# Early transposed tiles of a hybrid decoder layer: Newton steps on GpSimd, smaller pieces, and the next load behind the transposes

## The chip, the core and the metric

The kernel runs on one core of a Trainium2 chip. The core has five engines with queues of their own: TensorE (PE, matrix products; PEld is its weight load), VectorE (DVE), ScalarE (ACT), GpSimd (POOL) and SyncE (SP, which here only starts DMA transfers; ACT and POOL start some too). The metric is the device time of one execution in microseconds, lower is better. "Profile" is one execution recorded by the hardware profiler.

## The reference

One layer of a decoder with 2048 prompt rows and 8 sample rows of width 1024. A row is normalized by the root of its mean square, multiplied by a gain and shifted by a modulation worked out from a condition vector; then one input projection, a gated linear recurrence (LRU) group beside a gated linear attention (GLA) group of four heads, an output projection, a gate, the residual and a last normalization:

```
ada = jax.nn.silu(c) @ w_ada + b_ada
shift, scale, gate = jnp.split(ada, 3, axis=-1)
hn = _rmsnorm(x, g_norm) * (1.0 + scale[:, None]) + shift[:, None]
z = hn @ w_in
xa, za, q, k, v, glr, zg = jnp.split(z, SPLITS, axis=-1)
...
mix = jnp.concatenate([y_lru, y_gla], axis=-1) @ w_out
x = x + gate[:, None] * mix
```

What matters here is `hn`, and in it only the rows 1024 to 2047.

## The kernel before

The prompt is worked in two halves of 1024 rows. The first half's normalized rows lie on chip as a high and a low part (`hh`, `hl`), transposed, so that products can be made in three matmuls (L388 to L390 for the values of a head, L703 to L705 for all other projections, in `project`). A head of GLA makes the values of eight row tiles (`values`; ACT copies the high part out of the accumulator at L999, DVE subtracts for the low part at L1000, after which the accumulator is free; there are four accumulators), then keys and queries in two segments, with the decay (L1015 to L1054) between, the products of keys and queries (L1084 reads what DVE multiplies at L1069), and two segments of gates. An LRU tile makes two projections in segments (`xa_unit`, `za_unit`), with a convolution (L1321), a SiLU (L1172 on ACT, L1173 on DVE) and a scan (L1366 to L1377) at its end. The order in the first half is: head 3; LRU tile 0; head 0; LRU tiles 1, 2; head 1; LRU tiles 3, 4; head 2; LRU tiles 5, 6, 7.

**The early tiles.** While the first half is projected, the eight row tiles of the second half are made ready by `turn_ahead` (L263). It takes one tile of 128 rows at a time: load from memory (L266), sum of squares on ACT (L167), inverse root (`scales`, which calls `rsqrt`, L149 to L155: three preparing steps and three Newton rounds of three steps each, on one column), scaling of the rows (`times`, L183), transposes of 32 by 32 blocks into a second buffer (L277), a multiplication and an addition with the modulation (L284), and four stores to memory (L289). Both buffers come from a pool of two (`xt`). When the second half begins, `hn_load` (L296) reads all tiles back and `modulate` (L197, with L208 on POOL and L209 on DVE) splits them into high and low parts.

**What sets their order.** `after(units, f)` puts `f` on a list that is due so many units later; `tick` moves the clock, by 1 after a projection of a segment and by 0.5 after a row tile's values, and calls all that is due, in order of due time. A step that comes due between two ticks waits for the next. The tile steps are chained so: squaring 3 units after the load, scaling with transposes 0.5 later, both modulations 0.5 later, stores 0.5 later, and then the next tile's load. `behind(V)` (L723) keeps an instruction behind the last one traced on DVE so far. Beyond that, a scheduler at build time draws up each engine's queue: what is traced earlier goes first, but an instruction whose inputs are ready may pass earlier ones that are not.

In the same stretch of time other work hangs on the same clock: `pair_weights` (differences of weight blocks on DVE at L819 and L825, copies on ACT at L824, stores and loads by POOL at L827 and L815), then `out_weights` (L858, L893, loads and stores by POOL at L872 and L907), and the splitting of projection weights (L346 on ACT, L347 on DVE, stored by SP at L364). `apply` (L219), which works on the first rows, runs its copy on POOL (L229) and its subtraction on DVE (L232).

Of the kernel before, what the change touches and what calls it, by code (L numbers as in the profile page):

```python
# [8 lines left out]
F32 = mybir.dt.float32  # L9
# [3 lines left out]
OP = mybir.AluOpType  # L13

P = 128
D = 1024
KT = D // P
T = 2048
TH = T // 2
NS = 8  # L20
# [34 lines left out]
def hybrid_kernel(ctx, tc, i, o):  # L55
    nc = tc.nc
    V, S, G, PE, SP = nc.vector, nc.scalar, nc.gpsimd, nc.tensor, nc.sync
# [30 lines left out]
    xp = p1.enter_context(tc.tile_pool(name="xp", bufs=2))  # L88
# [52 lines left out]
                    mybir.DependencyClass.NoSync, mybir.DependencyReason.DATA), reason="in_order")  # L141
            last[x.engine] = x

    def rsqrt(pool, out, ss, n, rows, scale):

        y = pool.tile([P, 16], F32, tag="rs_y", name="rs_y", bufs=1)[:rows, :n]
        t = pool.tile([P, 16], F32, tag="rs_t", name="rs_t", bufs=1)[:rows, :n]
        x = pool.tile([P, 16], F32, tag="rs_x", name="rs_x", bufs=1)[:rows, :n]
        V.tensor_scalar(x, ss, scale, EPS, op0=OP.mult, op1=OP.add)  # L149
        V.tensor_scalar(t.bitcast(I32), x.bitcast(I32), 1, None, op0=OP.logical_shift_right)  # L150
        V.tensor_scalar(y.bitcast(I32), t.bitcast(I32), -1, 0x5F3759DF, op0=OP.mult, op1=OP.add)
        for it in range(3):
            V.tensor_tensor(t, y, y, op=OP.mult)
            V.scalar_tensor_tensor(t, t, -0.5, x, op0=OP.mult, op1=OP.mult)
            V.scalar_tensor_tensor(out if it == 2 else y, t, 1.5, y, op0=OP.add, op1=OP.mult)  # L155
# [9 lines left out]
    def square_sum(pool, out, x, m, n, tag="f512"):  # L165
        junk = pool.tile([P, 1024], mybir.dt.bfloat16, tag=tag, name="junk", bufs=2)
        S.activation(junk[:m, :n], x, AF.Square, accum_out=out)  # L167

    def squares(pool, xt, m=P, tag="f512", ss=None, j0=0):
        if ss is None:  # L170
            ss = pool.tile([P, 4], F32, tag="ss", name="ss", bufs=2)
        for j, x in enumerate(xt, j0):
            square_sum(pool, ss[:m, j:j + 1], x[:m], m, D, tag)
        return ss

    def scales(pool, ss, n, m=P):
        rs = pool.tile([P, 4], F32, tag="rs", name="rs", bufs=2)
        rsqrt(pool, rs[:m, :n], ss[:m, :n], n, m, 1.0 / D)
        return rs

    def times(xt, rs, m=P, j0=0):
        for j, x in enumerate(xt, j0):
            V.tensor_scalar(x[:m], x[:m], rs[:m, j:j + 1], None, op0=OP.mult)  # L183

    def normalize(pool, xt, m=P, tag="f512"):

        times(xt, scales(pool, squares(pool, xt, m, tag), len(xt), m), m)
# [74 lines left out]

    def turn_ahead(q, gm):  # L263

        x, w = [xp.tile([P, TH + NS], F32, tag="xt", name="xt")[:, :D] for _ in range(2)]
        SP.dma_start(x, i["x_prompt"][0, TH + q * P:TH + (q + 1) * P])  # L266

        def squared():
            ss = squares(xp, [x])
            after(0.5, lambda: scaled(ss))  # L270

        def scaled(ss):
            with behind(V):
                times([x], scales(xp, ss, 1))
                for h in range(2):
                    y, z = [v[:, 512 * h:512 * h + 512] for v in (w, x)]
                    V.transpose(y.rearrange("p (c k j) -> p c k j", c=4, k=4), z.rearrange("p (k c j) -> p c k j", c=4, k=4))  # L277
            after(0.5, modulated)

        def modulated():  # L280
            w3 = w.rearrange("p (b j) -> p b j", j=32)
            with behind(V):
                for n, op in enumerate((OP.mult, OP.add)):
                    V.tensor_tensor(w3, w3, gm[:, n, :, None].to_broadcast([P, 32, 32]), op=op)  # L284
            after(0.5, stored)

        def stored():
            for a in range(4):
                SP.dma_start(fd[q // 4, :, :, 4 * (q % 4) + a].rearrange("h (c r) f -> r (h c) f", c=4),  # L289
                             w[32 * a:32 * a + 32].rearrange("r (b f) -> r b f", b=8))  # L290
            if q < 7:
                turn_ahead(q + 1, gm)

        after(3, squared)

    def hn_load():  # L296

# [138 lines left out]
    rows = st.tile([NROW, D], F32, tag="rows", name="rows")  # L436
# [167 lines left out]
    def first_head():  # L604
# [29 lines left out]
        with in_order():  # L634
            ranks = []
            ss = squares(st, xt0[4:6], P, "junk")
            split_parts(1)
            rs = scales(st, ss, 2)
            split_parts(1)
            times(xt0[4:6], rs)  # L640
# [82 lines left out]
    def behind(q):  # L723

        return tc.issue_after(next(x for x in reversed(list(nc.cur_bb.bb.instructions)) if x.engine == q.engine))
# [17 lines left out]
    def after(units, fn, gla=False, val=False):  # L743
        clock[1] += 1
        heapq.heappush(pend, (clock[0] + units, clock[1], fn, gla, val))
# [17 lines left out]
    def ada_gate():  # L763

        pg = acc()

        def step(kt):
            ws = [xp.tile([P, TH + NS], F32, tag="xt", name="xt")[:, :D] for _ in range(2)]
            for n, w in enumerate(ws):
                SP.dma_start(w, i["w_ada"][0, (kt + n) * P:(kt + n + 1) * P, 2 * D:])  # L770

            def mm():
                for n in (1, 0):
                    for g in range(4):
                        PE.matmul(pg[32 * g:32 * g + 32, :256], sc[:, kt + n], ws[n][:, g * 256:(g + 1) * 256],
                                  start=kt == 0 and n == 1, stop=kt == KT - 2 and n == 0)
                if kt + 2 < KT:
                    step(kt + 2)
                else:
                    gr = xp.tile([P, 512], F32, tag="f512", name="gr")[:, :256]  # L780
                    S.copy(gr, pg[:, :256])
                    SP.dma_start(gated, gr)
                    after(4, lambda: ready("gate"))
                    turn_ahead(0, spread_modulation())
            after(3, mm)

        step(0)
# [339 lines left out]
    def gla_norm(nch, run):  # L1127
        _, on, ss = run
        rs = gp.tile([P, 4], F32, tag="ors", name="ors")
        rsqrt(gp, rs[:, :nch], ss[:, :nch], nch, P, 1.0 / DV)  # L1130
        for c in range(nch):
            V.tensor_scalar(on[:, c], on[:, c], rs[:, c:c + 1], None, op0=OP.mult)
# [21 lines left out]
    def sample_out(h, qm, s0, done):  # L1154

        os_ = gp.tile([P, DV], F32, tag="os", name="os")
        po = psum.tile([P, 512], F32, tag="o", name="po", bufs=1)[:, :DV]
        for m in range(2):
            for n in (3, 0, 1, 2):
                PE.matmul(po[32 * n:32 * n + 32], qm[:, 4 * m + n], s0[m][:, n], start=m == 0, stop=m == 1)  # L1160
        for m in range(2):
            G.dma_start(o[7][0, 4 * m:4 * m + 4, h].rearrange("b k v -> k b v"), s0[m])
        V.tensor_copy(os_, po)
        ss = gp.tile([P, 4], F32, tag="oss2", name="oss2")
        rs = gp.tile([P, 4], F32, tag="ors2", name="ors2")
        square_sum(xp, ss[:, :1], os_, P, DV)
        rsqrt(gp, rs[:, :1], ss[:, :1], 1, P, 1.0 / DV)
        V.tensor_scalar(os_, os_, rs[:, :1], None, op0=OP.mult)
        done(os_)
# [1047 lines left out]
    for n in range(2, 16):  # L2217
        g = n - 1
        x, prev = pairs[n], pairs[n - 1]
# [81 lines left out]
```

## Time and profile before

| | |
|---|---|
| median of 3 runs | 1453.01 us (1451.71 to 1453.09) |
| the profiled execution | 1452.74 us |
| its span, from the first to the last instruction | 1450.5 us |
| granted clock of TensorE, mean | 0.995 |
| instructions | 23542 |

A page of the profile gives busy times by engine and the costliest groups of instructions by line. Other views of the same trace give the waits of an engine (whom it waited for, total us, times, longest us) and the timeline: start in us from the span's start, duration in us, engine, line, operation, written and read tiles, shape, count, and in brackets the idle time of the engine just before, with what ended it. Times of the text are from the span's start.

### The profile page before, as it was taken

Reading aid. Unit: us, or ns where it says so; the run is one execution under the profiler, and the core shown is the slowest. Engines: PE = TensorE matmul, PEld = TensorE weight load, DVE = VectorE, ACT = ScalarE, POOL = GpSimd, SP = SyncE. Lnnn points to the kernel's source line nnn. Section 1 sums busy time; section 2 is a strip of 40 time slices with the busy share of each in tenths; the row PEclk is TensorE's granted clock in tenths of the full one; section 3 lists DMA queues with packets and bytes.
Section 4 is the critical chain, followed back from the end, with each engine's and each line's share of the span. In section 5 each row is a group of like instructions: output and inputs, shape, how many; then the busy total and the mean of one; then the engine's idle time right before and its main releaser. Section 6 shows DMA issues by size and latency. Waiting matters only on the chain.

```text
span 1450.5 us, 23542 instructions
## 1 busy us (share of the span) xinstructions
PE 1418.1 (98%) x8677; PEld 1246.9 (86%) x8677; DVE 1079.9 (74%) x2551; ACT 679.9 (47%) x1227; POOL 220.0 (15%) x362
## 2 busy tenths in 40 slices
PE   8999999989999999999999999999999999999998
PEld 6889989878888988888899999999998887778886
DVE  5757659877888768945458688596888986688886
ACT  4644544654366345524354454635567522144342
POOL 1200111121111114000110422333210000000000
PEclk9999999999999999999999999999999999999999
DMA  9755776885667667567744675665671767694453
GB/s 327 270 185 175 262 248 214 264 270 185 215 199 222 208 200 256 184 241 235 287 149 153 200 247 165 236 196 181 235 250 71 280 225 277 225 359 136 139 168 116
DMA packets 176840, 313.75 MB, mean 216 GB/s; under 512 B 20370, under 2 KB 106034, under 8 KB 173901
## 3 DMA queue, kind: packets, MB, share of 16 engines
q1 hardware_dynamic: 122821, 225.82, 46.0%
q0 software_dynamic: 22912, 70.96, 14.5%
q10 hardware_dynamic: 30992, 15.47, 3.6%
q8 instruction: 68, 1.11, 0.3%
q14 instruction: 47, 0.39, 0.1%
HBM read 192.74 MB, written 119.53 MB: 215 GB/s over the span
## 4 chain that ended last, share of the span: by engine, by line
PE 82%; DVE 9%; ACT 3%; DMA 3%; issue 2%; POOL 0%; DVEq 0%; SPq 0%; ACTq 0%
PE acc L1887 12%; PE acc L703 11%; PE acc L705 11%; PE acc L704 11%; PE tp L1887 9%; PE acc L1601 6%; PE acc L388 4%; PE acc L389 3%; PE acc L390 3%; PE po L1115 2%; DMA w<-parts 1%; DMA wada<-in_w_ada_dram 1%; PE acc L1358 1%; PE tp L1084 1%; PE tp L1206 1%
## 5 line engine op out<-in xcount | busy, mean ns | idle before, releaser
L703 PE MATMUL acc<-hh,w 128*128 128x512 f32 (+3 forms) x1112 | 378.0, 340 | 3.5 <-DVE zs L1173 1.9
L705 PE MATMUL acc<-hh,w 128*128 128x512 f32 (+3 forms) x1112 | 376.5, 339 | 0.0
L704 PE MATMUL acc<-hl,w 128*128 128x512 f32 (+3 forms) x1112 | 375.9, 338 | 0.0
L703 PEld LDWEIGHTS acc<-hh,w 128*128 128x128 f32 x1112 | 210.1, 189 | 21.3 <-issue 3.0
L705 PEld LDWEIGHTS acc<-hh,w 128*128 128x128 f32 x1112 | 210.0, 189 | 16.3
L704 PEld LDWEIGHTS acc<-hl,w 128*128 128x128 f32 x1112 | 210.0, 189 | 15.3
L1887 PE MATMUL acc<-w,a 128*128 128x512 f32 (+1 forms) x792 | 184.8, 387 | 0.0
L1887 PEld LDWEIGHTS acc<-w,a 128*128 128x128 f32 x792 | 146.8, 188 | 33.2 <-issue 3.4
L388 PE MATMUL acc<-w,hh 128*128 128x256 f32 (+1 forms) x508 | 145.0, 286 | 5.6 <-DVE vl L1000 5.4
L390 PE MATMUL acc<-w,hl 128*128 128x256 f32 (+1 forms) x508 | 143.5, 282 | 0.2 <-DVE hl L232 0.2
L389 PE MATMUL acc<-w,hh 128*128 128x256 f32 (+1 forms) x508 | 143.4, 282 | 0.0
L1887 PE MATMUL tp<-w,a 128*128 128x512 f32 x564 | 136.1, 391 | 0.0
L1887 PEld LDWEIGHTS tp<-w,a 128*128 128x128 f32 x564 | 105.2, 188 | 26.9 <-issue 5.2
L388 PEld LDWEIGHTS acc<-w,hh 128*128 128x128 f32 x508 | 96.5, 190 | 7.4 <-DVE vl L1000 6.0
L390 PEld LDWEIGHTS acc<-w,hl 128*128 128x128 f32 x508 | 96.6, 190 | 0.4 <-DVE hl L232 0.4
L389 PEld LDWEIGHTS acc<-w,hh 128*128 128x128 f32 x508 | 96.2, 189 | 0.2
L1172 ACT ACTIVATE zs<-acc 128x512 f32<-128x512 f32 (+3 forms) x70 | 34.3, 490 | 112.6 <-PE acc L705 105.7
L1737 ACT CAST a<-s 128x512 fp32r<-128x512 f32 x61 | 36.5, 620 | 94.7 <-issue 35.2
L1321 DVE SCALAR_TENSOR_TENSOR cv<-xa,vecT,cv 128x512 f32<-128x512 f32 (+2 forms) x120 | 76.2, 639 | 3.5 <-ACT cv L1319 2.9
L1173 DVE SCALAR_TENSOR_TENSOR zs<-zs,acc 128x512 f32<-128x512 f32 (+3 forms) x70 | 38.3, 548 | 35.6 <-ACT zs L1172 35.6
L999 ACT CAST vh<-acc 128x256 fp32r<-128x256 f32 x56 | 20.5, 370 | 87.6 <-PE acc L390 71.9
L1000 DVE TENSOR_TENSOR vl<-acc,vh 128x256 fp32r<-128x256 f32 x56 | 23.2, 418 | 47.0 <-ACT vh L999 46.9
(402 smaller groups left out, 2756.2 us busy)
## 6 DMA issues: line engine op xcount, KB each, us to landing
parts<-w SPq DMA_DIRECT2D x37, 1024.0 KB
w<-parts SPq DMA_DIRECT2D x28, 1024.0 KB
wr<-in_w_in_dram SPq DMA_DIRECT2D x38, 512.0 KB
a<-mixd SPq DMA_DIRECT2D x63, 256.0 KB
w<-wd SPq DMA_DIRECT2D x12, 1024.0 KB
w<-twd SPq DMA_DIRECT2D x20, 512.0 KB
wada<-in_w_ada_dram SPq DMA_DIRECT2D x16, 512.0 KB
mixd<-zs ACTq DMA_DIRECT2D x32, 256.0 KB
```

The source lines that it names most:

```text
L388: PE.matmul(ps, hh[:, kt, c], hi[:, kt % 4], start=kt == 0, stop=False)
L389: PE.matmul(ps, hh[:, kt, c], lo[:, kt % 4], start=False, stop=False)
L390: PE.matmul(ps, hl[:, kt, c], hi[:, kt % 4], start=False, stop=kt == KT - 1)
L703: PE.matmul(ps[:, :n], hi[:, kt], a, start=kt == 0, stop=False)
L704: PE.matmul(ps[:, :n], hi[:, kt], b, start=False, stop=False)
L705: PE.matmul(ps[:, :n], lo[:, kt], a, start=False, stop=kt == KT - 1)
L1172: S.activation(z, ps, AF.Tanh, scale=0.5)
L1173: V.scalar_tensor_tensor(z, z, 1.0, ps, op0=OP.add, op1=OP.mult)
L1321: V.scalar_tensor_tensor(cv[:, cq], xa[:, cq.start + k:cq.stop + k], cw[k], cv[:, cq], op0=OP.mult, op1=OP.add)
L1601: PE.matmul(ps, w[:, u, k], x[v][k], start=start and (k, u, v) == (0, 0, 0), stop=(k, u) == (3, 1), skip_group_check=True)
L1737: S.copy(t[:, 0, k], (low(t) if src is None else src)[:, k])
L1887: PE.matmul(ps, t[:, u, k], w[:, v, k, c], start=(q < 3 or ps is own) and (k, u, v) == (0, 0, 0), stop=(k, u) == (3, 1), skip_group_check= ...
```

## The change

The inverse root gets a parameter for the engine of its Newton rounds; for the early tiles these run on POOL, in four steps a round, where DVE took three. The root is made in the step that squares. The second buffer is taken only when the transposes are due. The step after that scales and transposes, and then starts the next tile (its load). The two modulations become steps of their own, and the stores follow. The distances are 3.5, 0.75, 0.5, 0.5 and 0.5 units.

```
-    def rsqrt(pool, out, ss, n, rows, scale):
+    def rsqrt(pool, out, ss, n, rows, scale, q=V):
...
         for it in range(3):
+            if q is G:
+                G.tensor_tensor(t, y, y, op=OP.mult)
+                G.tensor_tensor(t, t, x, op=OP.mult)
+                G.tensor_scalar(t, t, -0.5, 1.5, op0=OP.mult, op1=OP.add)
+                G.tensor_tensor(out if it == 2 else y, t, y, op=OP.mult)
+                continue
             V.tensor_tensor(t, y, y, op=OP.mult)
             V.scalar_tensor_tensor(t, t, -0.5, x, op0=OP.mult, op1=OP.mult)
             V.scalar_tensor_tensor(out if it == 2 else y, t, 1.5, y, op0=OP.add, op1=OP.mult)
...
     def turn_ahead(q, gm):
-        x, w = [xp.tile([P, TH + NS], F32, tag="xt", name="xt")[:, :D] for _ in range(2)]
+        x = xp.tile([P, TH + NS], F32, tag="xt", name="xt")[:, :D]
         SP.dma_start(x, i["x_prompt"][0, TH + q * P:TH + (q + 1) * P])
 
         def squared():
-            ss = squares(xp, [x])
-            after(0.5, lambda: scaled(ss))
-
-        def scaled(ss):
+            rs = scales(xp, squares(xp, [x]), 1, P, G)
+            after(0.75, lambda: turned(rs))
+
+        def turned(rs):
+            w = xp.tile([P, TH + NS], F32, tag="xt", name="xt")[:, :D]
             with behind(V):
-                times([x], scales(xp, ss, 1))
+                times([x], rs)
                 for h in range(2):
...
-            after(0.5, modulated)
-
-        def modulated():
+            if q < 7:
+                turn_ahead(q + 1, gm)
+            after(0.5, lambda: modulated(w, 0, OP.mult))
+
+        def modulated(w, n, op):
             w3 = w.rearrange("p (b j) -> p b j", j=32)
             with behind(V):
-                for n, op in enumerate((OP.mult, OP.add)):
-                    V.tensor_tensor(w3, w3, gm[:, n, :, None].to_broadcast([P, 32, 32]), op=op)
-            after(0.5, stored)
-
-        def stored():
+                V.tensor_tensor(w3, w3, gm[:, n, :, None].to_broadcast([P, 32, 32]), op=op)
+            after(0.5, (lambda: stored(w)) if n else lambda: modulated(w, 1, OP.add))
+
+        def stored(w):
             for a in range(4):
...
-            if q < 7:
-                turn_ahead(q + 1, gm)
-
-        after(3, squared)
+
+        after(3.5, squared)
```

More of the change, by code (lines that the diff above doesn't have):

```diff
@@ L174, in squares, with scales @@
         return ss
-    def scales(pool, ss, n, m=P):
+    def scales(pool, ss, n, m=P, q=V):
         rs = pool.tile([P, 4], F32, tag="rs", name="rs", bufs=2)
-        rsqrt(pool, rs[:m, :n], ss[:m, :n], n, m, 1.0 / D)
+        rsqrt(pool, rs[:m, :n], ss[:m, :n], n, m, 1.0 / D, q)
         return rs
```

## The prediction

> **What bounds the kernel now.** I read the engines' busy table first, then the waits of TensorE (PE) alone, then the order of time around the two largest of them.
>
> ```profile
> PE 1418.1 (98%) x8677; PEld 1246.9 (86%) x8677; DVE 1079.9 (74%) x2551; ACT 679.9 (47%) x1227; POOL 220.0 (15%) x362
> ```
>
> PE is busy for 98% of a span of 1450.5 us, so about 32 us in all can be gained by anything that leaves the matmuls as they are, and the change leaves them. DVE is at 74%: work taken from it is worth nothing by itself, only where PE stands for it. The early tiles run within 185 to 495 us. PE's waits there:
>
> ```profile
> PE acc L388 <- DVE vl L1000: 5.4, 1, 5.4
> PE tp L1084 <- DVE xb L1069: 3.1, 2, 2.1
> PE acc L1358 <- ACT xh L1345: 0.4, 1, 0.4
> PE acc L1359 <- DVE xl L1346: 0.4, 1, 0.4
> ```
>
> That is 9.3 us. One of the L1084 waits (1.0 us, at 188.73, quoted below with the other) lies ahead of the first tile's work, so 8.3 us is the most that easing the tiles can bring. Two stalls carry it: A, 5.4 us, and B, 2.1 us. Both have an early tile's pieces in front of them. Stall A, on DVE, with the line of ACT and of PE that belong to it:
>
> ```profile
> 286.70 0.69 DVE L1173 SCALAR_TENSOR_TENSOR zs<-zs,acc 128x512 f32<-128x512 f32 x1 [3.33 <-ACT zs L1172]
> 287.31 0.14 DVE L149 TENSOR_SCALAR rs_x<-ss 128x1 f32<-128x1 f32 x1
> ...
> 290.73 0.75 DVE L183 TENSOR_SCALAR xt<-xt,rs 128x1024 f32<-128x1024 f32 x1
> 292.82 1.23 DVE L347 TENSOR_TENSOR w<-wr,w 128x1024 fp32r<-128x1024 f32 x1 [1.34 <-DMA wgr<-in_w_gate_x_dram]
> 293.96 1.30 DVE L277 STREAM_TRANSPOSE xt<-xt 128x512 f32<-128x512 f32 x2
> 295.18 0.65 DVE L819 TENSOR_TENSOR tr<-tr 128x512 f32<-128x512 f32 x1
> ...
> 302.36 1.20 DVE L284 TENSOR_TENSOR xt<-xt,gm 128x1024 f32<-128x1024 f32 x1
> 303.48 0.14 DVE L1380 COPY hc<-tg 128x1 f32<-128x1 f32 x1
> ...
> 304.14 1.21 DVE L284 TENSOR_TENSOR xt<-xt,gm 128x1024 f32<-128x1024 f32 x1
> 305.27 1.28 DVE L825 TENSOR_TENSOR tr<-tr,th 128x512 f32<-128x512 f32 x2
> 306.48 0.41 DVE L1000 TENSOR_TENSOR vl<-acc,vh 128x256 fp32r<-128x256 f32 x1
> ```
>
> ```profile
> 296.47 0.35 ACT L999 CAST vh<-acc 128x256 fp32r<-128x256 f32 x1
> ```
>
> ```profile
> 306.95 0.58 PE L388 MATMUL acc<-w,hh 128*128 128x256 f32 x1 [5.42 <-DVE vl L1000]
> ```
>
> The subtraction that frees the accumulator (306.48) has had its input since 296.8. It is DVE's queue that is late: from 292.82 DVE works without a gap, and in that stretch lie tile 2's transposes and both its modulations. Ahead of it is slack: 3.33 us idle before 286.70 and 1.34 us before 292.82. Stall B:
>
> ```profile
> 327.32 0.14 DVE L149 TENSOR_SCALAR rs_x<-ss 128x1 f32<-128x1 f32 x1
> ...
> 327.88 0.16 DVE L153 TENSOR_TENSOR rs_t<-rs_y 128x1 f32<-128x1 f32 x1
> ...
> 329.62 0.75 DVE L183 TENSOR_SCALAR xt<-xt,rs 128x1024 f32<-128x1024 f32 x1
> 330.41 1.31 DVE L277 STREAM_TRANSPOSE xt<-xt 128x512 f32<-128x512 f32 x2
> 331.64 0.65 DVE L858 TENSOR_TENSOR g<-g,bt 128x512 f32<-128x512 f32 x1
> 332.21 0.68 DVE L1069 SCALAR_TENSOR_TENSOR xb<-acc,xb 128x512 f32<-128x512 f32 x1
> ```
>
> ```profile
> 188.73 1.16 PE L1084 MATMUL tp<-xb,e 128*128 128x128 f32 x8 [0.96 <-DVE xb L1069]
> ...
> 332.94 1.16 PE L1084 MATMUL tp<-xb,e 128*128 128x128 f32 x8 [2.14 <-DVE xb L1069]
> ```
>
> Tile 3's whole first piece (327.32 to 331.64, 4.32 us) stands in front of the product that PE waits for.
>
> **Part 1: where the pieces go.** I count the clock of units from the call that starts the gate weights. An LRU tile of two segments ticks 4, one with sample columns 6; a head ticks eight halves, then 4, then 4. Tile 0 starts at 12 in both kernels. Before, a tile's four steps come at 3, 3.5, 4 and 4.5 units, each put off to the next tick; after, at 3.5, 4.25, 4.75, 5.25 and 5.75, and the next tile starts at the second. So (scaling with transposes / first modulation / second) for tiles 0 to 7: before 16/17/17, 22/23/23, 28/28.5/28.5, 33/34/34, 39/40/40, 45/46/46, 50.5/51/51, 56/57/57; after 17/18/19, 22/23/24, 27/28/28.5, 31.5/32/33, 36/37/38, 41/42/43, 46/47/48, 50.5/51/51.5. The last store moves from 58 to 52; the load that reads these tiles back is due at 68, so that earliness is worth nothing.
>
> *Tile 2, stall A.* Transposes move from 28 to 27, into the 3.33 us idle before 286.70. The first modulation moves to where the root and scaling stood (from 287.31), ahead of the gapless stretch; the root and scaling that it replaces there took longer than it does. The stretch loses 1.22 us (293.96 to 295.18) and 1.12 us (302.36 to 303.48): 2.34 us. The second modulation stays.
>
> *Tile 3, stall B.* Only one modulation is due at 33, where 4.32 us stood: PE's product would come at 332.21 - 4.32 + 1.2 = 329.1, ahead of 330.8 (332.94 - 2.14), when PE asked. B goes whole: 2.14 us.
>
> **Part 2: the root on GpSimd (POOL).** It takes nine steps of DVE off each tile, 1.74 us (327.88 to 329.62), 72 in all. Except at B, where the move already takes them out, PE was not waiting for them: 0. It adds 12 POOL instructions a tile, 96 in all, of one column, and two hand-overs (DVE to POOL, POOL to DVE). No one-column arithmetic on POOL is in the trace. The nearest rows:
>
> ```profile
> L2286 POOL MEMSET const-float32-0.0<- 128x1 f32 x1 | 0.1, 98 | 0.2 <-issue 0.2
> ```
>
> ```profile
> L229 POOL TENSOR_SCALAR hh<-hnf x15: 610/621/1154, 25.6 to 69.7; 128x512 fp32r<-128x512 f32 x15
> L208 POOL TENSOR_SCALAR hh<-fs x10: 617/1047/1117, 569.8 to 580.1; 128x512 fp32r<-128x512 f32 x10
> ```
>
> ```profile
> 26.28 0.69 DVE L232 TENSOR_TENSOR hl<-hnf,hh 128x512 fp32r<-128x512 f32 x1 [0.47 <-POOL hh L229]
> 571.91 1.09 DVE L209 TENSOR_TENSOR hl<-fs,hh 128x512 fp32r<-128x512 f32 x1
> ```
>
> One instruction costs between 0.1 us (one column, nothing read) and 0.62 us (512 columns): a root of 1.2 to 7.4 us. By size it is nearest to the memset; with steps that wait for each other I take 0.2 us, 2.4 us a root. What covers it is the distance from the squaring to the scaling; the shortest in the trace is tile 1's:
>
> ```profile
> 246.59 1.05 ACT L167 ACTIVATE junk<-xt 128x1024 bf16<-128x1024 f32 x1
> ```
>
> ```profile
> 257.95 0.75 DVE L183 TENSOR_SCALAR xt<-xt,rs 128x1024 f32<-128x1024 f32 x1
> ```
>
> From 247.8, with its read-out, to 257.95: 10.2 us. So the root hides: 0.
>
> It isn't free for DVE. The same subtraction takes 0.69 us with POOL still and 1.09 us beside POOL's L208, which itself goes from 0.62 to 1.05: while both read SBUF, DVE loses 0.40 us per 0.62 us of POOL's own work. At 0.098 us that is 0.063 us an instruction, 0.76 us a root (from 0 to 4.8, if each cost the full 0.40). It counts in stall A, because tile 3's squaring was issued in that very stretch before and nothing holds it back now:
>
> ```profile
> 300.85 1.06 ACT L167 ACTIVATE junk<-xt 128x1024 bf16<-128x1024 f32 x1 [1.69 <-DMA xt<-in_x_prompt_dram]
> ```
>
> Behind it come the three preparing steps, now free to run at once: 0.56 us on DVE (327.32 to 327.88). Charge at A: 0.76 + 0.56 = 1.32 us.
>
> The Trainium skill, "SBUF — State Buffer", summary of rules for kernel authors, is harsher: a GpSimd operation that reads SBUF and a DVE operation with two SBUF inputs block each other fully, the second to issue waiting for the first to end. The rows above agree that both get slower; 1.09 is under 0.69 + 0.62, so not wholly in turn. By the rule the charge would be 12 x 0.098 + 0.56 = 1.7 us and the time 0.4 us longer.
>
> **Part 3: the next load right behind.** In the text the load moves ahead of two modulations and four stores. On SP it already stood there:
>
> ```profile
> 222.50 1.30 DVE L277 STREAM_TRANSPOSE xt<-xt 128x512 f32<-128x512 f32 x2
> ```
>
> ```profile
> 223.83 0.35 SPq L266 DMA_DIRECT2D xt<-in_x_prompt_dram  x1
> 229.18 1.86 SPq L289 DMA_DIRECT2D fd<-xt  x4
> ```
>
> The scheduler had drawn it up right behind the transposes, which end at 223.80. So this part changes little of SP's queue: 0. The load still waits for the transposes, with weight stores and loads queued behind it, and no wait of PE above ends with a DMA. The stores wait longer for their second modulation; behind them stand weight transfers of a later projection. If that cover were gone, a modulation's 1.2 us would be the cost.
>
> **Sum.** A: 2.34 - 1.32 = 1.02 us. B: 2.14 us. Together 3.2 us off the profiled execution of 1452.74 us (span 1450.5 and 2.24 around it): 1449.5 us. The median of the runs shown is 1453.01, 0.27 above that execution; I leave that out of the forecast. A measurement of this kernel can tell about 0.2%, 2.9 us, from no change, so the forecast lies just beyond it.
>
> **Rivals.**
>
> *1. Both stalls go.* The place of the 306.48 subtraction behind 13.7 us of other work is one of the scheduler's choices; with the pieces elsewhere it may stand earlier. Then 8.3 us less, at most: 1444.4, say 1445. For it: its input was there 9.7 us early. Against: the work ahead of it was traced earlier and keeps its rank.
>
> *2. The gain is used up.* POOL's 96 reads cost the full 0.40 us each, so A gains nothing (2.34 - 4.8 - 0.56 = -3.0), or a modulation, now due at 48 where the next head begins as at A, makes a new stall of about its own 1.2 us. With B's 2.14 this gives 1452 (between 1451 and 1454). For it: DVE is gapless for 13 us at A. Against: one column is far from 512.
>
> *3. DVE waits for POOL (slower).* POOL serves its queue in order, and in front of a root can stand transfers that wait themselves:
>
> ```profile
> 281.75 0.89 POOL L815 DMA_DIRECT2D tr<-in_w_in_dram  x1 [3.93 <-issue]
> ...
> 447.43 0.54 POOL L907 DMA_DIRECT2D wd<-t  x1 [0.16 <-DVE rs_t L153]
> 449.18 1.56 POOL L872 DMA_DIRECT2D r<-in_w_out_dram  x2 [1.21 <-DMA wd<-r]
> ```
>
> With 0.62 us an instruction (7.4 us) behind 4 to 5 us of such transfers the root takes about 12 us, over the 10.2 us: DVE then stands some 2 us at each scaling, with the evictions of accumulators behind it. It decides where the root exceeds about 10 us. If 8 x 2 us reach PE less than half, 7 us are lost against 3.2 gained: 1456.5. For it: tile 7's root is due where POOL's transfers of 447 to 451 us stand. Against: 0.62 us is the price of 512 columns.
>
> **How the numbers follow.** Forecast 0.33 (its own range 1447.5 to 1450.1); rival 1 0.15; rival 2 0.32; rival 3 0.20. Faster by over 0.2% is the forecast and rival 1: 0.48; within, rival 2: 0.32; slower, rival 3: 0.20. The range of 1444.5 to 1456.5 takes in rivals 1 and 2 and half of rival 3.
>
> **What would show it.** In the trace after: no wait at L1084 near 330 us and the L388 wait near 307 us down to some 4 us; tile 2's transposes near 283 us; one-column POOL rows of about 0.1 to 0.2 us, and no idle DVE before L183 put down to POOL. Idle DVE there would prove rival 3; two-input DVE rows longer beside POOL by 0.4 us, rival 2. The forecast is wrong if new waits of PE come up between 185 and 495 us, or if a stretch after 495 us, where no work changed, is reordered.

## The result and the profile after

The changed kernel takes 1454.82 us (median of 20 runs, 1452.32 to 1462.82) against 1450.80 us of the kernel before, run beside it (20 runs, 1448.39 to 1453.09): a ratio of 1.0034 [1.0025, 1.0042], slower by 4.0 us in the medians and 5.0 us in the means. In three of the comparisons further down one run far out of line is left out (2835 us of e1, 8002 us of e10, 1554 us of e4; the cause is not known).

The lines of the changed kernel are those of before plus 6 from L153 on; within `turn_ahead` the transposes are L284 and the modulations L292. The engines' busy table of after:

```profile
PE 1423.6 (97%) x8677; PEld 1251.4 (86%) x8677; DVE 1071.9 (73%) x2479; ACT 678.5 (46%) x1227; POOL 245.3 (17%) x458
```

DVE has 72 instructions and 8 us less, as the change says, and POOL 96 more. PE's busy time grew by 5.5 us for the same 8677 matmuls, in a span of 1461.0 us: time went into waits, and into a lower clock (last section). The profiled execution is the longest of the 20; part of its excess has nothing to do with the change. The first early tile's load, ahead of which nothing was changed, and the first matmul of the second half, in the timeline of before:

```profile
187.40 0.34 SPq L266 DMA_DIRECT2D xt<-in_x_prompt_dram  x1
609.13 0.39 PE L1601 MATMUL acc<-hh,w 128*128 128x512 f32 x1
```

and of after:

```profile
189.68 0.34 SPq L272 DMA_DIRECT2D xt<-in_x_prompt_dram  x1
619.28 0.39 PE L1607 MATMUL acc<-hh,w 128*128 128x512 f32 x1
```

2.3 us are lost before the first tile, 10.2 us at the start of the second half: the stretch in between, where the early tiles run, lost 7.9 us in this execution. PE's waits in it (185 to 495 us, after):

```profile
PE tp L1090 <- DVE xb L1075: 7.5, 2, 6.6
PE tp L1212 <- DVE on L1138: 3.5, 1, 3.5
PE acc L394 <- DVE zs L1179: 2.7, 1, 2.7
PE acc L1365 <- DVE xl L1352: 0.2, 1, 0.2
```

13.9 us where before had 9.3. Stall A (L394 for a value's low part) is gone; two waits have come up that before did not have, at L1212 and at L394, and the one at L1090 (B's place) has tripled. Each is a wait for DVE, and DVE itself stands idle where it did not before. DVE's waits, 190 to 480 us, after; neither row has a counterpart before:

```profile
DVE xt L189 <- POOL rs L157: 13.2, 3, 6.9
DVE tr L825 <- DMA tr<-in_w_in_dram: 4.8, 1, 4.8
```

The first row is the scaling of a tile waiting for its root, the second a subtraction of pair weights waiting for its load. In order of time, each of the three long waits of PE comes behind such a stand of DVE: the one that ends at 229.25 behind the stand for the load (to 219.62), those that end at 300.30 and 340.41 behind two for the root (6.87 us to 297.58, 4.82 us to 324.36). Tile 2's root, on DVE and on POOL in the timeline of after:

```profile
285.72 0.14 DVE L149 TENSOR_SCALAR rs_x<-ss 128x1 f32<-128x1 f32 x1
...
288.84 0.15 DVE L151 TENSOR_SCALAR rs_y<-rs_t 128x1 int32<-128x1 int32 x1
...
297.58 0.75 DVE L189 TENSOR_SCALAR xt<-xt,rs 128x1024 f32<-128x1024 f32 x1 [6.87 <-POOL rs L157]
```

```profile
287.65 0.91 POOL L821 DMA_DIRECT2D tr<-in_w_in_dram  x1 [5.15 <-DMA twd<-tr]
293.43 0.90 POOL L821 DMA_DIRECT2D tr<-in_w_in_dram  x1 [4.86 <-issue]
294.34 0.20 POOL L154 TENSOR_TENSOR rs_t<-rs_y 128x1 f32<-128x1 f32 x1
...
297.36 0.19 POOL L157 TENSOR_TENSOR rs<-rs_t,rs_y 128x1 f32<-128x1 f32 x1
```

The root's input is there at 288.99. POOL begins at 294.34, because its queue has the two loads of the next pair weights in front, and between them it stands for 4.86 us with nothing in the profile to explain it. The root itself takes 3.2 us (294.34 to 297.55). DVE, whose queue is served in order, stands for 6.87 us behind it.

### The profile page after: what moved, and what is told of

Same layout as the page of the kernel before. It is cut to its first block, busy times and chain, and to the rows that moved or that the text cites. A ratio compares the mean times of both kernels' runs of the same rounds, so it can differ in the third digit from the quotient of the medians.

```text
span 1461.0 us, 23574 instructions
## 1 busy us (share of the span) xinstructions
PE 1423.6 (97%) x8677; PEld 1251.4 (86%) x8677; DVE 1071.9 (73%) x2479; ACT 678.5 (46%) x1227; POOL 245.3 (17%) x458
## 4 chain that ended last, share of the span: by engine, by line
PE 75%; DVE 9%; issue 6%; ACT 4%; DMA 4%; SPq 1%; POOL 1%; DVEq 0%; POOLq 0%; ACTq 0%
PE acc L1893 12%; PE acc L709 10%; PE acc L711 10%; PE acc L710 10%; PE tp L1893 9%; PE acc L1607 6%; PE acc L394 3%; PE acc L396 3%; PE acc L395 3%; PE po L1121 2%; DMA w<-parts 1%; PE tp L1212 1%; PE acc L1364 1%; PE tp L1090 1%; DMA tr<-in_w_in_dram 1%
## 5 line engine op out<-in xcount | busy, mean ns | idle before, releaser
L394 PE MATMUL acc<-w,hh 128*128 128x256 f32 (+1 forms) x508 | 145.0, 285 | 3.0 <-DVE zs L1179 2.7
L394 PEld LDWEIGHTS acc<-w,hh 128*128 128x128 f32 x508 | 96.3, 190 | 4.7 <-DVE zs L1179 2.9
L352 ACT CAST w<-wr 128x1024 fp32r<-128x1024 f32 (+2 forms) x40 | 41.1, 1027 | 29.5 <-DMA wr<-in_w_in_dram 19.0
```

What stands on the lines that cost most here:

```text
L352: split += [lambda r=r: S.copy(hi[:, r], raw[:, r]), lambda r=r: V.tensor_tensor(lo[:, r], raw[:, r], hi[:, r].bitcast(F32), op=OP.subtract)]
L394: PE.matmul(ps, hh[:, kt, c], hi[:, kt % 4], start=kt == 0, stop=False)
```

## The experiments

The expectations speak of these theories. **Theory 1**: the root is late because POOL is late with it, and DVE waits. **Theory 2** (also "rival 2", contention): POOL's one-column steps slow the DVE work beside them. **Theory 3**: the load right behind the transposes changed SP's queue. In all, moved pieces, root, pair loads (L821) and the due time of the pair subtractions (L825) were switched one by one. Each ratio is to the kernel before, run beside it; the rows were taken in several groups on different chips, so a difference between two rows is one of such ratios. PE's waits are those of the profiled execution, and 0.96 us of them lie ahead of the first tile's work (188 to 191 us) in all but e10, e14 and e15:

| | pieces | root | pair loads on | subtractions after | ratio | PE waits 185 to 495 us |
|---|---|---|---|---|---|---|
| before | old | DVE | POOL | 4 | 1 | 9.3 |
| e2 | old | POOL | POOL | 4 | 1.0081 [1.0068, 1.0094] | 19.8 |
| e1 | moved | DVE | POOL | 4 | 1.0010 [1.0001, 1.0019] | 8.5 |
| after | moved | POOL | POOL | 4 | 1.0034 [1.0025, 1.0042] | 13.9 |
| e9 | old | DVE | SP | 4 | 0.9982 [0.9974, 0.9991] | 7.9 |
| e8 | moved | DVE | SP | 4 | 0.9946 [0.9931, 0.9961] | 3.9 |
| e6 | moved | POOL | SP | 4 | 0.9983 [0.9974, 0.9992] | 5.1 |
| e15 | old | DVE | POOL | 5 | 0.9990 [0.9981, 1.0000] | 7.9 |
| e10 | moved | DVE | POOL | 5 | 0.9936 [0.9923, 0.9949] | 2.9 |
| e14 | moved | POOL | POOL | 5 | 0.9984 [0.9975, 0.9994] | 6.9 |

### e1: the root back on DVE

```
-            rs = scales(xp, squares(xp, [x]), 1, P, G)
+            rs = scales(xp, squares(xp, [x]), 1)
```

> All of the change, but the root's nine steps back on DVE. SP's queue is in the same order as with the change. Theory 1 (the root on POOL comes late, because POOL's queue is held by its own transfers, and DVE stands for it: 13.2 us in three tiles): the waits of DVE at the scaling are gone, the PE stalls of 2.7 us near 300 and 6.6 us near 340 us are under 2.5 us each, and the time is 1447 to 1451 us, at or under before (1450.8). Theory 2 (the new places of the pieces and of the load are the cause): the time stays at 1453.5 to 1456 us. A smaller part that either theory leaves: the 3.5 us stall near 229 us, where DVE stands 4.75 us for a load of pair weights, should stay.

1.0010, 1453.0 us, between the ranges of the two theories: some 3.5 us of the loss are the root's. But the moved pieces alone are no gain either. The largest of PE's waits, and the DVE row ahead of it, in the traces of e1:

```profile
PE acc L394 <- DVE vl L1006: 4.5, 1, 4.5
```

```profile
298.12 0.69 DVE L825 TENSOR_TENSOR tr<-tr 128x512 f32<-128x512 f32 x1 [5.83 <-issue]
```

Stall A is still 4.5 us, and now because DVE, done earlier with the tile's transposes, stands for 5.83 us in front of the first subtraction of a pair of weights. B fell from 2.14 to 0.81 us. The profile names no releaser for DVE's wait; ahead of it stands the second of two loads, which POOL held, and e8 and e10 below remove the wait by way of that load:

```profile
283.57 0.92 POOL L821 DMA_DIRECT2D tr<-in_w_in_dram  x1 [4.84 <-DMA twd<-tr]
289.08 0.90 POOL L821 DMA_DIRECT2D tr<-in_w_in_dram  x1 [4.60 <-issue]
```

### e2: the root on POOL and nothing else

```
-                times([x], scales(xp, ss, 1))
+                times([x], scales(xp, ss, 1, P, G))
```

> The kernel before with only the root's Newton steps on POOL; places, pieces and load as before. Theory 1: the root now starts right ahead of the scaling that needs it, 12 steps at 0.27 us are 3.3 us and more where POOL's transfers stand in front, so DVE waits at the scaling in most of the eight tiles (20 us or more in all) and the time is 1454 to 1462 us, slower than before by 3 us or more. Theory 2: 1450 to 1452 us, no slower than before, because nothing was moved.

1.0081, 1463.8 us, the worst of all and above the range of theory 1. Here the root is begun in the step that scales, without a lead, and DVE waits at nearly every tile (DVE's waits, 190 to 480 us):

```profile
DVE xt L189 <- POOL rs L157: 20.7, 7, 5.7
```

### e3: squaring a unit earlier

```
-            after(0.75, lambda: turned(rs))
+            after(1.75, lambda: turned(rs))
...
-        after(3.5, squared)
+        after(2.5, squared)
```

> The change, with the squaring and root due one unit earlier (2.5 in place of 3.5) and the scaling where it was (1.75 behind in place of 0.75). Theory 1: a unit is about 5.5 us, so DVE's waits of 6.9, 4.8 and 1.5 us at the scaling fall to about 1.4, 0 and 0, and the time to 1449 to 1452.5 us, if the load lands in time. Theory 2: scaling, modulations and load are where they were, so it stays at 1453.5 to 1456 us.

This expectation failed: 1.0059 [1.0041, 1.0078], slower still. Two of the three waits at the scaling are gone, as expected. But tile 2's root is again behind the second pair load. POOL in the timeline of e3:

```profile
279.45 0.92 POOL L821 DMA_DIRECT2D tr<-in_w_in_dram  x1 [5.06 <-DMA twd<-tr]
287.70 0.90 POOL L821 DMA_DIRECT2D tr<-in_w_in_dram  x1 [7.33 <-issue]
288.61 0.21 POOL L154 TENSOR_TENSOR rs_t<-rs_y 128x1 f32<-128x1 f32 x1
```

DVE stands for 9.9 us at that one scaling, the longest of any run. So at tile 2 it isn't the due time that makes the root late but its place in POOL's queue. A second loss goes with the earlier squaring itself: DVE reaches the first preparing step before ACT has squared and stands for 4.1 us (to 327.07), and behind that PE waits for 5.6 us in B's place.

### e5: the next load behind the stores again

```
-        def stored(w):
...
+        def stored(w, then):
...
+            if then:
+                then()
```

> The change with the next tile's load issued behind the stores again; all due times as with the change. Theory 3 (SP stands at the load until the scaling and transposes are done, and the weight transfers behind it come late; the load of weights near 331 us came 7 us later than before): the weight loads near 320 to 331 us come in time, the stall near 340 us falls under 3 us, and the time is 1451 to 1453 us. Theory 1 alone: the waits for POOL stay and the time is 1453.5 to 1457 us, or longer, since the root starts later still.

1.0021 [1.0010, 1.0033], which overlaps with the changed kernel's interval; DVE's wait for POOL is the same 13.2 us. Theory 3 carries nothing that these runs can tell from zero (the difference is 1.9 us, and about as uncertain).

### e6, e8, e9: the pair loads off POOL's queue

```
-            G.dma_start(r[:, a], i["w_in"][0, :, col:col + P].rearrange("(k p) n -> p k n", p=P))
+            SP.dma_start(r[:, a], i["w_in"][0, :, col:col + P].rearrange("(k p) n -> p k n", p=P))
```

in the changed kernel (e6), in e1 (e8) and in the kernel before (e9).

> The change, with the ten loads of pair weights issued by SP in place of POOL. Theory 1, made sharper (what makes the root late is the second load of each pair, which holds POOL's queue 5 to 10 us; a unit more of head start did not help because the root stands behind that load whenever it is due): the 6.9 us wait of DVE at the scaling near 298 us goes, the one near 324 us (behind other loads) may stay, DVE's 4.8 us for the pair weights near 220 us goes, and the time is 1448 to 1452 us. Theory 2 (places of the pieces): no change against the change itself, 1454 to 1456 us.

> Root back on DVE and the pair loads on SP. If the pair loads of POOL are what is left of the loss without POOL's root (DVE stood 5.8 us at a subtraction of pair weights ahead of the 4.5 us stall near 305 us, and another time ahead of the 2.0 us stall near 224 us): both stalls under 1.5 us and 1446 to 1450 us, under before. If the places are the cause: 1452 to 1454 us.

> The kernel before with only the pair loads moved to SP: control for the two runs above. In before, DVE never stood for a pair load, so theory 1 expects little: 1449 to 1452 us. If the move helps by itself (weights come earlier) it is 1447 or less, and the gain of the two runs above is not the change's; if it hurts (SP held at the pair loads), 1453 or more.

With the ten loads off POOL's queue the changed kernel drops from 1.0034 to 0.9983. In the kernel before the same edit gives 0.9982, 2.6 us less, a little more than theory 1 had. The moved pieces with the root on DVE, a loss of 0.1% in e1, are now worth 0.36% (e8 against e9, 5.2 us), and e8 is at 1443.3 us, below its expected range. PE's waits of e9, then of e8:

```profile
PE acc L388 <- DVE vl L1000: 4.0, 1, 4.0
PE tp L1084 <- DVE xb L1069: 3.1, 2, 2.2
```

```profile
PE tp L1090 <- DVE xb L1075: 3.1, 2, 2.1
```

Stall A is gone altogether, B is not (2.1 us of the 3.1). The root on POOL still costs 0.37% (e6 against e8, 5.4 us): DVE's waits of e6, with the row of tile 3, between whose root steps POOL issues other loads (L858 to L878, after the third of the twelve steps):

```profile
DVE xt L189 <- POOL rs L157: 8.6, 3, 4.9
```

```profile
312.65 0.76 DVE L189 TENSOR_SCALAR xt<-xt,rs 128x1024 f32<-128x1024 f32 x1 [4.92 <-POOL rs L157]
```

### e12: the same POOL steps with nobody waiting

e8, and behind the root on DVE:

```
+            u, v = rs[:, 1:2], rs[:, 0:1]
+            for it in range(3):
+                G.tensor_tensor(u, v, v, op=OP.mult)
+                G.tensor_tensor(u, u, v, op=OP.mult)
+                G.tensor_scalar(u, u, -0.5, 1.5, op0=OP.mult, op1=OP.add)
+                G.tensor_tensor(u, u, v, op=OP.mult)
```

> The kernel of e8 (root on DVE, pair loads on SP) with twelve more POOL instructions a tile behind the root: the same twelve one-column steps as the changed kernel's root, on a column that nobody reads. They add work and leave out none; no engine waits for them. The base measured 0.9946 of before (1443.3 us). Theory 1 (the root costs because DVE waits for its result): nothing waits here, so the ratio stays within 0.9930 to 0.9960 and PE's waits between 185 and 495 us stay under 5 us. Rival 2 (the root costs because POOL's reads slow DVE's work beside it, up to 0.40 us a step): the 5.7 us by which e6 stood above e8 come back whatever the result is used for, so 0.9970 to 0.9985 (some 1447 to 1449 us), with two-input DVE rows of 0.69 us at 0.9 us and more beside the steps.

0.9950 [0.9936, 0.9964] beside e8's 0.9946: 96 POOL steps with no one waiting cost nothing that can be told, and the 0.9970 of contention lies outside. One part of the expectation failed: PE's waits in the profiled execution, the longest of the six at 1448.46 us, are 7.2 us in place of under 5, 5.5 of them at L1096, B's place; ahead of it DVE had stood for 3.27 us for ACT's half of a weight split (L359). DVE's own work did not get longer. The modulations in the groups by line, of e12 and of e8 (in e12 two of the sixteen have POOL steps beside them, and take 1.21 us each):

```profile
L298 DVE TENSOR_TENSOR xt<-xt,gm 128x1024 f32<-128x1024 f32 x16 | 19.5, 1216 | 0.0
```

```profile
L292 DVE TENSOR_TENSOR xt<-xt,gm 128x1024 f32<-128x1024 f32 x16 | 19.5, 1216 | 0.0
```

### e13, e4: the root on POOL, given more room

e13 is e6 with the squaring 0.75 units earlier and the scaling where it was; e4 is e6 with POOL's loads for the output projection (L858, L859, L878) on SP as well.

```
-            after(0.75, lambda: turned(rs))
+            after(1.5, lambda: turned(rs))
...
-        after(3.5, squared)
+        after(2.75, squared)
```

```
-            G.dma_start(g, dram(gated, (8 + 32 * q) * 256, [[0, P], [64 * 256, 2], [1, 256]]))
+            SP.dma_start(g, dram(gated, (8 + 32 * q) * 256, [[0, P], [64 * 256, 2], [1, 256]]))
...
```

> The kernel of e6 (root on POOL, pair loads on SP) with the squaring 0.75 units earlier (2.75 in place of 3.5) and the scaling where it was (1.5 behind the squaring in place of 0.75). e6 measured 0.9983, e8 with the root on DVE 0.9946. Theory 1 (waiting for the root's end): POOL's queue is free of pair loads, so the longer lead is now used, unlike in e3: DVE's waits for POOL at L189 between 190 and 480 us fall from 8.6 us to under 3 us and the ratio to 0.9945 to 0.9970. Rival 2 (contention): the number of POOL steps is the same, the ratio stays at 0.9975 to 0.9995. A third way: the earlier squaring makes DVE's three preparing steps wait in front of other work, as in e3; then waits of DVE for ACT's junk at L149 grow by 2 us or more and the ratio is above 0.9985.

> The changed kernel (root on POOL) with the pair loads and the output projection's loads of weights, gate and bias (L821, L858, L859, L878) on SP in place of POOL. What is left on POOL are stores and the root. e6, with the pair loads alone moved, measured 0.9983 and had one DVE wait for POOL of 4.9 us near 312 us, behind the output projection's loads. Theory 1 (POOL's own loads in front of the root): that wait falls under 3 us and the total of DVE's waits for POOL at L189 from 8.6 to under 6 us; ratio 0.9955 to 0.9980. Rival 2 (contention): as e6, 0.9975 to 0.9990. Rival of SP's queue: the loads, each waiting for its buffer, hold up the other weights on SP; then PE gets waits that end with a DMA or with ACT's casts behind 300 us, and the ratio is 0.9990 to 1.0030.

0.9971 [0.9961, 0.9982] and 0.9970 [0.9956, 0.9984]. DVE's waits of e13, then of e4:

```profile
DVE xt L189 <- POOL rs L157: 5.4, 2, 3.7
DVE rs_x L149 <- ACT junk L173: 5.2, 4, 2.7
```

```profile
DVE xt L189 <- POOL rs L157: 4.8, 3, 2.5
```

In e4 the wait behind the output projection's loads went as theory 1 had it. In e13 the waits fell from 8.6 to 5.4 us only, not under 3, and the earlier squaring has DVE wait for ACT 2.4 us more than in e6 (2.8 us), as the third way had it. The lead in e13 did grow: DVE's last preparing step ends 5.5 and 3.3 us ahead of the moment when DVE is free for the scaling, at tiles 2 and 3. But the roots take 7.0 and 6.8 us there, at tile 2 with steps of up to 1.72 us and at tile 3 with the other loads between the steps. Both kernels lie between e6 and e8, but their intervals overlap with e6's; that the rest of the root's price is this lateness alone is likely from the waits and not shown by the times.

### e10, e14, e15: the pair subtractions a unit later

```
-        after(4, lambda: one([[sub(b11, b12, b11), sub(b12, b22, b12), sub(b22, b22, b11), sub(b21, b21, b22)],
+        after(5, lambda: one([[sub(b11, b12, b11), sub(b12, b22, b12), sub(b22, b22, b11), sub(b21, b21, b22)],
```

in e1 (e10), in the changed kernel (e14) and in the kernel before (e15).

> The kernel of e1 (moved pieces, root on DVE, pair loads on POOL) with the subtractions of the pair weights due a unit later (5 in place of 4 units behind their call), so that the second pair load, which POOL holds, has more time to land. e1 measured 1.0010 and PE's wait at L394 near 309 us was 4.5 us, with DVE standing 5.8 us for the pair load in front of it. If that standing is what ate the moved pieces' gain at stall A: DVE's wait for the pair load falls under 2 us, the L394 wait to 0 to 2.5 us, ratio 0.9965 to 0.9990. If something else holds DVE there (its total of work in the stretch): the L394 wait stays at 3.5 us or more and the ratio within 1.0000 to 1.0020. If the pair weights themselves get late for the matmuls that use them: a new PE wait of 2 us or more behind 310 us, and the ratio over 1.0020.

> The changed kernel (moved pieces, root on POOL, pair loads on POOL) with the subtractions of the pair weights due a unit later. With the root on DVE this measured 0.9936; the changed kernel itself 1.0034. Theory 1 (the root stands in POOL's queue behind the pair loads, whose hold does not depend on the subtractions' due time): DVE still waits at L189 for POOL by 6 us or more in sum between 190 and 480 us, its wait for the pair load at L825 falls from 4.8 us to under 2 us, and the ratio lies from 0.9965 to 1.0005, some 4 to 10 us over the same kernel with the root on DVE. Rival (the standing at the pair load was the whole loss, and the root's lateness is covered): ratio 0.9925 to 0.9955.

> Control: the kernel before with nothing but the subtractions of the pair weights a unit later. In the trace of before DVE waits for no pair load at all. Theory 1 (the later subtractions help only the moved pieces, which made DVE reach the subtractions too early): within 0.9980 to 1.0015 of before, stalls A and B still there with 4 us or more in sum. Rival (the later subtractions themselves take work out from in front of stall A, whatever the pieces do): A falls under 2.5 us and the ratio is 0.9940 to 0.9975, so that most of e10's gain is not the moved pieces'.

e10 is the best kernel of all, 0.9936, below every expectation. DVE waits for no pair load, and all of PE's waits between 185 and 495 us are:

```profile
PE tp L1090 <- DVE xb L1075: 1.8, 1, 1.8
PE acc L1365 <- DVE xl L1352: 0.8, 1, 0.8
PE tp L1212 <- DVE on L1138: 0.3, 1, 0.3
```

The control e15 is at 0.9990, with A at 3.9 us and B at 2.4:

```profile
PE acc L388 <- DVE vl L1000: 3.9, 1, 3.9
PE tp L1084 <- DVE xb L1069: 2.4, 1, 2.4
```

So the later subtractions give the old order next to nothing, and the moved pieces are worth 0.54% beside them (e10 against e15, 7.8 us). In e14, where DVE waits for no pair load either, the root on POOL takes most of that back (0.9984, 7.0 us over e10): it is a loss of its own, not only through DVE's standing for the pair loads. DVE's waits of e14:

```profile
DVE xt L189 <- POOL rs L157: 6.5, 3, 3.1
```

## Why the prediction was wrong

The forecast was 3.2 us faster; the measured change is 4 to 5 us slower, near rival 3's 3.8. The mechanism is rival 3's, with transfers in POOL's queue in front of the root, but not on its terms.

**The step that failed is Part 2's cover: "From 247.8, with its read-out, to 257.95: 10.2 us. So the root hides: 0."** It counts from the squaring on ACT to the scaling. But the root begins with what DVE's three preparing steps leave, and these stand in DVE's own queue; the prediction took them as "now free to run at once". Tile 2's squaring in after:

```profile
277.16 1.06 ACT L173 ACTIVATE junk<-xt 128x1024 bf16<-128x1024 f32 x1
```

With its read-out it is done at 278.3. DVE, at work without a gap, ends the third preparing step at 288.99, and it is free for the scaling at 290.71 (297.58 less the 6.87 us of waiting; rows above). From squaring to scaling that is 12.4 us, even more than forecast, but the cover of the root itself is 1.7 us. At tile 3 it is 1.9 us of 11.3; at the five tiles where DVE does not wait it is 4.8 us or more. At tiles 2 and 3 the root doesn't fit in even with nothing in front of it on POOL, as e6 shows, where POOL begins tile 2's root 0.15 us behind the last preparing step (281.45) and ends it at 285.55:

```profile
281.15 0.15 DVE L151 TENSOR_SCALAR rs_y<-rs_t 128x1 int32<-128x1 int32 x1
...
285.58 0.75 DVE L189 TENSOR_SCALAR xt<-xt,rs 128x1024 f32<-128x1024 f32 x1 [2.55 <-POOL rs L157]
```

**The wait in POOL's queue**, which rival 3 named, comes on top. At tile 2 of after the second pair load stands in front of the root, and 5.4 us of the 8.6 between the last preparing step and the end of the root are waiting, not work. Rival 3 asked for a step price of 0.62 us before it would decide; with so little cover it decided at 0.19.

**The size of the root** was too small in the sum as well, though the step price was right: 0.2 us a step was forecast, and the timings of after's L154 (least, median and longest, in ns) give 0.19 us:

```profile
L154 POOL TENSOR_TENSOR rs_t<-rs_y x24: 185/193/1254, 215.7 to 444.4; 128x1 f32<-128x1 f32 x24
```

But a step starts only every 0.27 us, so a root takes 3.2 us at the least, where 2.4 were forecast, and up to 6.7 us in after, where single steps get long or, at tile 3, other loads come between them. With everything else equal the root on POOL costs 3.5, 5.4, 7.0 and 11.8 us (after against e1, e6 against e8, e14 against e10, e2 against before).

**Part 1** was right in kind and too small where nothing is in the way: A was to lose 2.34 us of work and in e8 and e10 goes whole, as rival 1 had it. In e1 that gain does not come, for a wait that no part of the sum held: with its pieces elsewhere DVE reaches the pair subtractions before their second load is there (5.83 us ahead of A in e1; 4.75 us in after, at an earlier pair; none before). e10 with its control e15 shows this. In after DVE stands for tile 2's root in A's place. B, which was to go whole, fell to 0.81 us in e1 but is 2.1 us in e8 and 1.8 us in e10: there PE, with A gone, asks for the product at 323 or 322 us (331 before), before DVE has done the modulation and the other work in front of it. That a stall taken away lets PE run into the next one earlier was not in the sum.

**The charge for contention** (0.76 of the 1.32 us at A) was on the wrong engine. e12 shows no price on DVE. It is POOL that waits, here in e6 for the rest of a DVE instruction with two inputs:

```profile
337.84 1.05 POOL L156 TENSOR_SCALAR rs_t<-rs_t 128x1 f32<-128x1 f32 x1
```

```profile
337.61 1.22 DVE L353 TENSOR_TENSOR w<-wr,w 128x1024 fp32r<-128x1024 f32 x1
```

The step begins 0.23 us behind the DVE instruction and ends within 0.1 us of it, and DVE's 1.22 us are what L353 takes with no POOL instruction beside it, too (at 289.50 in after). This agrees with the rule of the Trainium skill that the prediction cited ("SBUF — State Buffer", summary of rules for kernel authors: the second to issue waits for the first to end). What the prediction missed is who comes second: a POOL step is over in 0.19 us, a DVE instruction of two inputs takes 0.7 to 1.2, so POOL is mostly the one that runs into the other. In after 14 of the 96 steps take over 0.35 us, and each of them overlaps a DVE instruction with two inputs. The price then is a longer root, not a slower DVE.

**Part 3**, the load at 0, stands as far as e5 can tell, which is to some 2 us.

**What the prediction said would prove rival 3**, idle DVE before the scaling put down to POOL, is the first row of DVE's waits in after. Rival 2's sign, two-input DVE rows longer by 0.4 us beside POOL, did not show.

## What to carry to other kernels

Work given to another engine's queue is priced by what stands in front of it there, transfers above all, and not by its own length; read that queue in the trace at the very time at which the work will come due. A cover counts from the end of the last step that feeds the work, not from the start of the chain: here the chain left 12.4 us, and DVE's own queue took all but 1.7 of them. And when an eased engine gains nothing, look at what it now reaches too early: here, with the root on DVE, one due time a unit later turned +0.10% into -0.64%.

## What the runs showed of the hardware

**A stall can cost more than its length.** After the long waits of after PE runs at a lower granted clock. The three waits of after in the timeline, with the windows behind the first (busy us and count of PE, PEld, DVE, ACT and POOL, then the granted clock):

```profile
229.25 1.17 PE L1212 MATMUL tp<-ident,on 128*128 128x128 f32 x4 [3.50 <-DVE on L1138]
...
300.30 0.58 PE L394 MATMUL acc<-w,hh 128*128 128x256 f32 x1 [2.71 <-DVE zs L1179]
...
340.41 2.08 PE L1090 MATMUL tp<-xb,e 128*128 128x128 f32 x8 [6.58 <-DVE xb L1075]
```

```profile
229.25:231.00 1.75, 1.75 (x9) 1.57 (x9) 1.51 (x5) 0.18 (x1) 0.00 (x0) 0.50 0.00 0
231.00:233.00 2.00, 2.00 (x10) 1.82 (x8) 2.00 (x5) 1.03 (x2) 1.29 (x3) 0.50 0.47 133
233.00:235.00 2.00, 2.00 (x11) 2.00 (x11) 2.00 (x4) 0.19 (x1) 1.41 (x3) 0.50 0.82 289
235.00:237.00 2.00, 2.00 (x17) 2.00 (x17) 0.98 (x4) 0.00 (x0) 0.00 (x0) 0.92 1.08 338
```

For nearly 6 us behind a wait of 3.50 us the clock is 0.50, and PE makes about half as many matmuls. The eight small matmuls of L1090 take 2.08 us where they took 1.16 before. Over whole stretches, before and then after:

```profile
185.00:250.00 65.00, 63.91 (x398) 56.41 (x397) 48.74 (x134) 31.20 (x65) 11.37 (x19) 1.00 0.71 230
250.00:305.00 55.00, 50.70 (x311) 44.87 (x310) 48.90 (x96) 32.60 (x50) 8.75 (x14) 1.00 0.77 246
```

```profile
185.00:250.00 65.00, 60.54 (x356) 53.28 (x355) 43.86 (x106) 26.56 (x53) 14.14 (x32) 0.95 0.68 220
250.00:305.00 55.00, 52.05 (x295) 45.84 (x295) 46.15 (x100) 32.64 (x53) 14.78 (x38) 0.97 0.74 234
```

0.05 of 65 us and 0.03 of 55 us are about 4.9 us of clock at most, beside 4.6 us more of waits: together enough for the 7.9 us that the stretch lost in this execution. From 305 to 345 us the clock is 0.91 in both kernels, so what the stalls of before cost in clock there, the third wait of after costs as well. The Trainium skill, "TensorE: Matmul & The Clock Gate", Part 1: The HAM clock gate, has the clock at half after an idle window of about 3.4 us and at full again after as long a busy one. The traces agree in kind; here a wait of 2.71 us was enough (0.54 from 300 to 302 us), and the way back took nearly 6 us behind the first. It isn't the wait's length alone: behind 2.11 us of waiting in e8 the eight matmuls of L1090 took 1.16 us, behind 1.81 us in e10 they took 1.97. What else decides was not tried.

**POOL's second pair load begins late.** In before, after and e1 alike the second of two loads of 512 KB issued from POOL begins some 5 to 10 us behind the first, with an idle time that no releaser explains (4.60 and 4.86 us in the rows above, 9.6 us at most). Whatever stands behind it on POOL is late by as much. Why the queue holds it wasn't tried apart.
